# One more buffer for split weights, in place of 15 KB of descriptor scratch, in a hybrid decoder block

## The chip, the core and the metric

The kernel runs on one NeuronCore of one Trainium2 chip. The metric is the device time of one execution in microseconds. The engines are named as in the profile: PE is the matrix engine (PEld its weight loads), DVE the vector engine, ACT the scalar engine, POOL the GpSimd engine, SP the engine that issues most of the transfers. Each engine works through its own list of instructions in order, and an instruction waits until the results and the buffers that it needs are signalled ready.

## The reference, cut to what matters

The reference computes one decoder layer for 256 tokens of width 1024, in float32. A normalised input goes through one wide projection into: a gated convolution (31 taps per channel, then a layer norm, a SiLU and a projection), a sparse attention with compressed, selected and windowed branches (16 heads in 4 groups), and two gates. The gated sum is projected and added to the input. Then come a cross-attention with 4 heads into 256 memory tokens, a SwiGLU feed-forward part of inner width 2816, and a final norm.

```python
h = rms_norm(x, norm_mix_g)
x = x + hybrid_mixer(h, w_in, conv..., cmp..., w_out, rel_bias)
h = rms_norm(x, norm_x_g)
x = x + cross_attention(h, mem, xq_w, xkv_w, xo_w)
h = rms_norm(x, norm_ffn_g)
x = x + swiglu(h, ffn_in_w, ffn_out_w)
return rms_norm(x, final_norm_g)
```

Nearly all of the weights, 95 MB read from HBM in the profile, pass through the core once.

## The kernel before, in words

**The products.** A float32 matrix is split into two parts of a shorter float format (`float32r`): a high part, which is the value rounded by a copy, and a low part, which is what the copy left. A product of two matrices is then three matmuls: high by high, high by low and low by high. The activations are split once and stay. The weights are split piece by piece as they arrive.

**A piece of weight** is 128 partitions by 1024 floats, 512 KB. Three steps make it ready: SP issues its load into a buffer of the kind `w` (line 203, or 211 for the last projection), ACT copies it into a buffer of the kind `whi` (line 174, tiles named `..._0h` or `..._1h`), and DVE subtracts the copy from the loaded piece into a buffer of the kind `wlo` (line 175, tiles `..._0l`, `..._1l`). The loaded piece is free once DVE has subtracted; the two parts are free once PE has used them. Before the change there are 3 buffers of the kind `w` and 4 each of `whi` and `wlo`. A chunk such as `kw` or `f7` is two pieces, 0 and 1. Some chunks (`q0` to `q3`, `kc`) are used as loaded, in full float32 (line 269); for them PE frees the `w` buffer.

**The stages**, in the order of the program: the keys of the memory (`k0` to `k3`), the convolution's input (`u0` to `u7`), the compressed keys and values and the queries (`kc`, `vc`, `q0` to `q3`), the keys and values of the two other branches (`ks`, `kw`, `vs`, `vw`), the gates (`ga0` to `ga3`, `gc0` to `gc3`) and the memory's values (`v0` to `v3`) interleaved with the attention, the projections `pw`, `wo`, `xq`, `xo`, the feed-forward input (22 chunks `f0` to `f21`, lines 1079 and 1081) and the feed-forward output (22 pieces `fo`, line 1108).

**Convolution.** The taps of the eight channel blocks are shared out: DVE accumulates some blocks in a PSUM tile `yp` by multiply-adds (line 405), and its last one writes `part`. ACT and POOL do the others: ACT multiplies (line 419, tiles `vw_...`), POOL multiplies some (417) and adds all (421). The taps are recorded with a low priority, so that they fill time which the engines have left. The last accumulating tile `yp` and the second tile of the compressed scores (`cs_ps`, line 679) share one PSUM buffer, so PE can begin the second half of the compressed scores only after DVE's last tap.

**Order.** The order on each engine is not written out: a scheduler in the framework replays the program against its own estimate of the times and the free buffers, and fixes the order on every engine when the program is built. So a change in the number of buffers moves instructions on all engines. On PE the stages from `ks` to the end of the attention are tied down by explicit order marks (`in_line`, `last`).

## Time and profile before

| | before |
|---|---|
| median of 3 timed runs | 566.5 us (564.79 to 567.01) |
| profiled execution, first to last instruction (its span) | 563.2 us |
| PE / PEld busy | 552.7 us (98%) / 507.0 us |
| DVE / ACT / POOL busy | 426.4 / 364.0 / 136.0 us |
| granted PE clock, mean | 0.997 |
| read from HBM, mean rate | 95.39 MB, 172 GB/s with the writes |

The profile is one execution. Its span runs from the first to the last instruction on the core; the timed runs contain what lies around it too, and the profile gives no time of its own for that. The busy time of PE is modelled at the ends of the matmuls, and a matmul overlaps the next one, so the distance between two starts, not the duration, is what one costs in a row of equal ones.

### The profile page before, as it was taken

What the parts mean: (1) busy time and instruction counts of PE and PEld (TensorE: products, weight loads), DVE (VectorE), ACT (ScalarE), POOL (GpSimd) and SP (SyncE); (2) the same over time, 40 slices, a digit from 0 to 9 for tenths busy, and PEclk for the clock granted to TensorE, in tenths of its full rate; (3) what the DMA queues carried; (4) which work ended last, traced back from release to release, by engine and by line L of the source; (5) the groups of instructions that cost most, each with busy time, mean ns of one, the idle gap of its engine ahead of it and who ended that gap; (6) DMA issues with size and microseconds to landing.
All of it is one profiled execution on the core that took longest, in us unless ns stands there. A gap on an engine that the chain in (4) does not pass through costs nothing.

```text
span 563.2 us, 10246 instructions
## 1 busy us (share of the span) xinstructions
PE 552.7 (98%) x3886; PEld 507.0 (90%) x3886; DVE 426.4 (76%) x779; ACT 364.0 (65%) x686; POOL 136.0 (24%) x123
## 2 busy tenths in 40 slices
PE   8999999999999999999999999999999999999995
PEld 7999998899899998998999999988888888888884
DVE  3888999899989788886678676587787878774541
ACT  4768658878966878779556655576655666554431
POOL 0006997999982000300003100140000000000000
PEclk9999999999999999999999999999999999999998
DMA  8837924446364463432665533535565655667632
GB/s 305 355 124 263 313 55 127 133 140 216 131 208 149 154 179 104 132 105 93 251 192 179 193 120 100 181 129 186 185 200 166 218 166 166 210 190 217 190 112 74
DMA packets 29153, 97.30 MB, mean 173 GB/s; under 512 B 3120, under 2 KB 5424, under 8 KB 28848
## 3 DMA queue, kind: packets, MB, share of 16 engines
q1 hardware_dynamic: 28384, 95.34, 51.8%
q10 hardware_dynamic: 720, 1.31, 0.6%
q8 instruction: 30, 0.49, 0.3%
q14 instruction: 19, 0.16, 0.1%
HBM read 95.39 MB, written 1.25 MB: 172 GB/s over the span
## 4 chain that ended last, share of the span: by engine, by line
PE 88%; DVE 4%; ACT 3%; DMA 2%; issue 2%; ACTq 0%
PE ps_f L1079 15%; PE fo L1108 11%; PE ps_u L239 8%; PE ps_f L1081 7%; PE ps_pw L239 4%; PE ps_v L239 4%; PE ps_xq L239 4%; PE ps_wo L239 4%; PE ps_xo L239 4%; PE ps_gc L239 4%; PE ps_k L239 3%; PE ps_ga L239 3%; PE ps_q L269 3%; DVE yp L405 2%; PE s L718 2%
## 5 line engine op out<-in xcount | busy, mean ns | idle before, releaser
L421 POOL TENSOR_TENSOR yt<-yt,vw 128x512 f32<-128x512 f32 x61 | 92.3, 1514 | 54.1 <-DMA u<-in_wst_dram 46.4
L405 DVE SCALAR_TENSOR_TENSOR yp<-vt,ppt,yp 128x256 f32<-128x256 f32 x108 | 52.3, 486 | 2.9
L1079 PE MATMUL ps_f<-g,f_1h 128*128 128x512 f32 x176 | 49.0, 397 | 0.0
L419 ACT ACTIVATE vw<-vt,ppt 128x256 f32<-128x256 f32 x104 | 44.3, 497 | 5.6 <-POOL yt L421 5.5
L1079 PE MATMUL ps_f<-g,f_0h 128*128 128x512 f32 x176 | 47.7, 396 | 0.0
L1150 POOL TENSOR_SCALAR x<-x,rr 128x512 f32<-128x512 f32 x1 | 0.7, 698 | 180.9 <-DVE rr L1120 180.9
L1079 PEld LDWEIGHTS ps_f<-g,f_1h 128*128 128x128 f32 x176 | 32.6, 188 | 7.2
L175 DVE TENSOR_TENSOR f_0l<-f,f_0h 128x1024 fp32r<-128x1024 f32 x22 | 27.5, 1250 | 14.4 <-ACT f_0h L174 8.7
L1079 PEld LDWEIGHTS ps_f<-g,f_0h 128*128 128x128 f32 x176 | 30.4, 188 | 4.3
L174 ACT ACTIVATE f_1h<-f 128x1024 fp32r<-128x1024 f32 x22 | 23.2, 1055 | 14.0 <-DMA f<-in_wst_dram 14.0
L174 ACT ACTIVATE f_0h<-f 128x1024 fp32r<-128x1024 f32 x22 | 23.3, 1060 | 13.6 <-PE ps_xo L239 3.6
L175 DVE TENSOR_TENSOR f_1l<-f,f_1h 128x1024 fp32r<-128x1024 f32 x22 | 26.9, 1221 | 6.6 <-ACT f_1h L174 6.6
L1081 PEld LDWEIGHTS ps_f<-g,f_0l 128*128 128x128 f32 x176 | 27.0, 189 | 3.9
L269 PE MATMUL ps_q<-hf,q 128*128 128x256 f32 x128 | 28.5, 381 | 0.0
L1081 PE MATMUL ps_f<-g,f_0l 128*128 128x256 f32 x176 | 28.3, 282 | 0.0
L1081 PE MATMUL ps_f<-g,f_1l 128*128 128x256 f32 x176 | 28.0, 281 | 0.0
L269 PEld LDWEIGHTS ps_q<-hf,q 128*128 128x128 f32 x128 | 24.1, 190 | 3.3
L1081 PEld LDWEIGHTS ps_f<-g,f_1l 128*128 128x128 f32 x176 | 24.0, 188 | 0.0
L738 ACT ACTIVATE p<-p,mins 128x256 f32<-128x256 f32 x32 | 15.9, 498 | 9.0 <-DVE mins L723 9.0
L1082 ACT ACTIVATE ab<-ps_f 128x256 f32<-128x256 f32 x44 | 16.2, 374 | 7.2 <-PE ps_f L1081 6.9
L1083 DVE TENSOR_TENSOR ab<-ps_f,ab 128x256 f32<-128x256 f32 x44 | 17.9, 418 | 1.5 <-ACT ab L1082 1.5
L283 ACT ACTIVATE uh<-sl 128x256 fp32r<-128x256 f32 x22 | 9.1, 413 | 11.1 <-DVE sl L1087 11.1
(540 smaller groups left out, 1559.6 us busy)
## 6 DMA issues: line engine op xcount, KB each, us to landing
f<-in_wst_dram SPq DMA_DIRECT2D x44, 512.0 KB
fo<-in_wfo_dram SPq DMA_DIRECT2D x22, 512.0 KB
u<-in_wst_dram SPq DMA_DIRECT2D x14, 512.0 KB
q<-in_wst_dram SPq DMA_DIRECT2D x8, 512.0 KB
ga<-in_wst_dram SPq DMA_DIRECT2D x8, 512.0 KB
gc<-in_wst_dram SPq DMA_DIRECT2D x8, 512.0 KB
v<-in_wst_dram SPq DMA_DIRECT2D x8, 512.0 KB
pw<-in_wst_dram SPq DMA_DIRECT2D x8, 512.0 KB
```

Of the source, the lines that this page charges most:

```text
L174: copy = nc.scalar.activation(hi, w, AF.Copy)
L175: splits[name] = copy, nc.vector.tensor_tensor(out=lo, in0=w, in1=f(hi[:]), op=ALU.subtract)
L239: mm = nc.tensor.matmul(ps[:, b], lhsT=lhsT, rhs=rhs, start=row + b + kb == 0, stop=kb == NB - 1 and row == 2 and b == 1)
L269: mm = nc.tensor.matmul(ps[:, b], lhsT=w[:, k, cs], rhs=x[:, kb], start=kb + b == 0, stop=kb == NB - 1 and b == 1)
L405: nc.vector.scalar_tensor_tensor(out=out[:, i] if t == ts[-1] else acc[:, i], in0=v, scalar=w, in1=acc[:, i], op0=ALU.mult, op1=ALU.add)
L419: nc.scalar.activation(pr[:, i], v, AF.Identity, scale=w, bias=col(PP_DB, j + i) if t == 0 else 0.0)
L421: nc.gpsimd.tensor_tensor(out=y, in0=y, in1=pr, op=ALU.add)
L1079: nc.tensor.matmul(ps, lhsT=hs[kb // 4][0][:, kb % 4, cs], rhs=fg[:, :, kb], start=kb == 0, stop=False)
L1081: nc.tensor.matmul(ps[:, 1], lhsT=hs[kb // 4][1][:, kb % 4, cs], rhs=fg[:, 0, kb], start=False, stop=kb == NB - 1)
L1082: nc.scalar.activation(ab[:, b], ps[:, 0], AF.Copy)
L1083: nc.vector.tensor_tensor(out=ab[:, b], in0=ps[:, 1], in1=ab[:, b], op=ALU.add)
L1108: nc.tensor.matmul(accs[c][tb], lhsT=t, rhs=w[:, k], start=False, stop=kb == NF - 1 and t is tl)
```

## The change

The scratch that is set aside at the start of SBUF for the descriptors of dynamic transfers shrinks from 16 KB to 1 KB per partition. The 15 KB hold three more buffers of 4 KB per partition: a fourth `w`, a fifth `whi` and a fifth `wlo`. No instruction is added or removed.

```diff
     def split(w, shape, name):
-        hi = small(f"{name}h", shape, F32R, tag="whi", bufs=4)
-        lo = small(f"{name}l", shape, F32R, tag="wlo", bufs=4)
+        hi = small(f"{name}h", shape, F32R, tag="whi", bufs=5)
+        lo = small(f"{name}l", shape, F32R, tag="wlo", bufs=5)
...
-        w = small(f"{name}_{i}", [P, 4, 256], tag="w", bufs=3)
+        w = small(f"{name}_{i}", [P, 4, 256], tag="w", bufs=4)
...
     def half(src, name):
-        w = small(name, list(src.shape), tag="w", bufs=3)
+        w = small(name, list(src.shape), tag="w", bufs=4)
...
-    nc = _bacc.Bacc("TRN2", target_bir_lowering=False, num_devices=1)
+    nc = _bacc.Bacc("TRN2", target_bir_lowering=False, num_devices=1, dynamic_dma_scratch_size=1024)
```

The scheduler, given the buffers, writes another order. On PE nothing moves until the feed-forward input; on ACT and DVE the split of a piece stands about one piece earlier from the `u` chunks on.

The first place is DVE in front of the keys `kw`. `yp` is the accumulator of the taps, `ks_0l` to `kw_1l` are the low parts of the pieces, `qt` the queries from the last `q` chunk, `kcp` the compressed keys.

```order
 L284 TENSOR_TENSOR kcp<-kc_ps,kcp 128x4x16
-L405 SCALAR_TENSOR_TENSOR yp_1191<-vt_354,ppt,yp_1191 128x256 x4
-L175 TENSOR_TENSOR ks_0l<-ks_1433,ks_0h 128x1024
-L405 SCALAR_TENSOR_TENSOR yp_1191<-vt_354,ppt,yp_1191 128x256 x4
+L405 SCALAR_TENSOR_TENSOR yp_1191<-vt_354,ppt,yp_1191 128x256 x3
 L175 TENSOR_TENSOR ks_1l<-ks_1463,ks_1h 128x1024
+L405 SCALAR_TENSOR_TENSOR yp_1191<-vt_354,ppt,yp_1191 128x256
+L175 TENSOR_TENSOR kw_0l<-kw_1512,kw_0h 128x1024
+L405 SCALAR_TENSOR_TENSOR yp_1191<-vt_354,ppt,yp_1191 128x256
+L175 TENSOR_TENSOR kw_1l<-kw_1542,kw_1h 128x1024
 L405 SCALAR_TENSOR_TENSOR yp_1191<-vt_354,ppt,yp_1191 128x256
 L558 SCALAR_TENSOR_TENSOR qt<-ps_q_1381,qt 64x256
```

Both low parts of `kw` now stand ahead of the queries of the last `q` chunk; before, they stood behind them. `ks_0l` moved further up, ahead of these rows.

The second place is ACT in front of the gates. `ga_...` are the pieces of the gates (1771 and 1801 belong to `ga0`, 1836 and 1879 to `ga1`, 1964 and 2035 to `ga2`), `kdh` and `vals` hold keys and values.

```order
 L419 ACTIVATE vw_22_1507<-vt_353,ppt 128x256 x2
-L174 ACTIVATE vs_1h<-vs_1603 128x1024
-L174 ACTIVATE vw_0h<-vw_1647 128x1024
-L174 ACTIVATE vw_1h<-vw_1677 128x1024
+L174 ACTIVATE ga_0h<-ga_0_1771 128x1024
 L576 ACTIVATE kdh<-ps_kw 64x2x256 x4
+L174 ACTIVATE ga_1h<-ga_1_1801 128x1024
+L174 ACTIVATE ga_0h<-ga_0_1836 128x1024
 L592 ACTIVATE vals<-ps_vs 128x2x256
```

The first copy for the gates now stands ahead of the keys of `kw`; before, it stood behind them, behind `vals` and behind four taps more. In the same stretch, a little later, the taps end on DVE:

```order
+L405 SCALAR_TENSOR_TENSOR yp_1191<-vt_354,ppt,yp_1191 128x256 x4
+L175 TENSOR_TENSOR ga_1l<-ga_1_1879,ga_1h 128x1024
 L405 SCALAR_TENSOR_TENSOR yp_1191<-vt_354,ppt,yp_1191 128x256 x2
-L175 TENSOR_TENSOR ga_1l<-ga_1_1879,ga_1h 128x1024
-L405 SCALAR_TENSOR_TENSOR yp_1191<-vt_354,ppt,yp_1191 128x256 x3
-L405 SCALAR_TENSOR_TENSOR part_361<-vt_354,ppt,yp_1191 128x256
 L175 TENSOR_TENSOR ga_0l<-ga_0_1964,ga_0h 128x1024
-L405 SCALAR_TENSOR_TENSOR part_361<-vt_354,ppt,yp_1191 128x256
+L405 SCALAR_TENSOR_TENSOR yp_1191<-vt_354,ppt,yp_1191 128x256 x4
+L405 SCALAR_TENSOR_TENSOR part_361<-vt_354,ppt,yp_1191 128x256 x2
 L175 TENSOR_TENSOR ga_1l<-ga_1_2035,ga_1h 128x1024
```

On DVE the same instructions as before stand ahead of the last tap (`part`), in another order: `ga_0l` of `ga2` stood between its two halves and stands six multiply-adds ahead of its end now.

The third place is PE in the feed-forward input. `ps_f_0_4823` is the first half of the outputs of chunk `f4`, `ps_f_0_4766` and `ps_f_1_4785` the two halves of `f3`; the same pattern is repeated for each following pair of chunks up to `f19` and `f20`.

```order
 L1079 MATMUL ps_f_0_4823<-g_3829,f_0h 128x512 x4
+L1079 MATMUL ps_f_0_4823<-g_3829,f_1h 128x512 x4
+L1081 MATMUL ps_f_0_4823<-g_3829,f_0l 128x256 x4
 L1079 MATMUL ps_f_0_4766<-g_3829,f_0h 128x512 x4
 L1079 MATMUL ps_f_0_4766<-g_3829,f_1h 128x512 x4
 L1081 MATMUL ps_f_0_4766<-g_3829,f_0l 128x256 x4
 L1081 MATMUL ps_f_0_4766<-g_3829,f_1l 128x256 x4
+L1081 MATMUL ps_f_0_4823<-g_3829,f_1l 128x256 x4
 L1079 MATMUL ps_f_1_4785<-g_3829,f_0h 128x512 x4
 L1079 MATMUL ps_f_1_4785<-g_3829,f_1h 128x512 x4
 L1081 MATMUL ps_f_1_4785<-g_3829,f_0l 128x256 x4
 L1081 MATMUL ps_f_1_4785<-g_3829,f_1l 128x256 x4
```

Twelve of the sixteen matmuls of the later chunk's first half now stand in front of the earlier chunk; before, only four did.

## The prediction, on record before the result was known

> **What bounds the kernel now.** I read the page's busy times and its chain of waits first, then the busy time by stage, then the gaps of PE one by one, and last who ended them. From the page:

> ```profile
> span 563.2 us, 10246 instructions
> ...
> PE 552.7 (98%) x3886; PEld 507.0 (90%) x3886; DVE 426.4 (76%) x779; ACT 364.0 (65%) x686; POOL 136.0 (24%) x123
> ...
> PE 88%; DVE 4%; ACT 3%; DMA 2%; issue 2%; ACTq 0%
> ```

> The last line is the head of the chain that ended last: it runs on PE for 88%. More buffers can give back only time in which PE waits, so I look for that. The columns of the next rows (busy time in stretches of the span) are the stretch, its length, then the busy time and count of PE, PEld, DVE, ACT and POOL, the clock, the DMA share and GB/s. The last row is a stretch that I chose later: from the queries of the second `q` chunk to the end of the taps.

> ```profile
> 100.00:120.00 20.00, 20.00 (x149) 17.58 (x149) 18.18 (x43) 16.12 (x40) 18.52 (x18) 1.00 0.41 134
> 120.00:140.00 20.00, 19.11 (x146) 18.43 (x145) 19.30 (x22) 16.95 (x33) 19.27 (x15) 1.00 0.56 190
> 140.00:160.00 20.00, 18.83 (x158) 17.58 (x157) 16.92 (x21) 15.74 (x27) 19.13 (x13) 1.00 0.48 164
> 160.00:180.00 20.00, 19.33 (x162) 18.95 (x161) 18.65 (x47) 14.02 (x31) 10.09 (x6) 1.00 0.50 165
> 180.00:200.00 20.00, 20.00 (x167) 18.78 (x166) 16.97 (x59) 15.72 (x45) 0.00 (x0) 1.00 0.45 143
> ...
> 382.00:492.00 110.00, 110.00 (x629) 96.09 (x627) 85.16 (x135) 66.85 (x116) 0.00 (x0) 1.00 0.58 186
> ...
> 112.95:164.24 51.29, 48.62 (x367) 45.72 (x365) 46.73 (x63) 41.57 (x79) 47.20 (x34) 1.00 0.50 170
> ```

> PE is full at 100, from 180 on and through the feed-forward input (382 to 492). Apart from the first loads, which the change does not touch, and the end, I found gaps only from 120 to 180. There DVE (46.73 of 51.29) and POOL (47.20) are nearly full too. The gaps in PE's own timeline (start, duration, instruction, count, and in brackets the idle time before it):

> ```profile
> 129.58 1.11 PE L239 MATMUL ps_kw<-hh,kw_0h 128*128 128x256 f32 x8
> 130.53 1.11 PE L239 MATMUL ps_kw<-hl,kw_0h 128*128 128x256 f32 x8
> 132.53 1.21 PE L239 MATMUL ps_kw<-hh,kw_0l 128*128 128x256 f32 x8 [0.89 <-DVE kw_0l L175]
> ...
> 150.77 1.21 PE L239 MATMUL ps_ga<-hh,ga_0h 128*128 128x256 f32 x8 [1.02 <-ACT ga_0h L174]
> 151.82 1.10 PE L239 MATMUL ps_ga<-hl,ga_0h 128*128 128x256 f32 x8
> 153.07 1.21 PE L239 MATMUL ps_ga<-hh,ga_0l 128*128 128x256 f32 x8
> ...
> 161.04 1.19 PE L239 MATMUL ps_ga<-hh,ga_1h 128*128 128x256 f32 x8
> 162.07 0.51 PE L679 MATMUL cs_ps<-kcp,qt 128*128 128x32 f32 x4
> 162.44 1.19 PE L239 MATMUL ps_ga<-hl,ga_1h 128*128 128x256 f32 x8
> 164.29 0.62 PE L679 MATMUL cs_ps<-kcp,qt 128*128 128x32 f32 x4 [0.67 <-DVE part L405]
> ```

> Eight matmuls take 0.95 us from start to start (129.58 to 130.53). So `kw_0l` came 132.53 - 130.53 - 0.95 = 1.05 us late, `ga_0h` 1.02, and `ga_0l` 153.07 - 151.82 - 0.95 = 0.30. In front of the compressed scores the same eight took 1.85 (162.44 to 164.29) instead of 1.03 (161.04 to 162.07): 0.82. Together 3.19 us. The first three wait for split weights, the last for DVE's last tap.

> **The change, part by part.**

> *The waits for weights.* `kw_0l` is late because it stands on DVE behind the four query parts of the last `q` chunk; the new order puts it and `kw_1l` ahead of them. `ga_0h` is late because ACT makes it after eight tap multiplications; now it is made before `kdh`. Both need their loads sooner, and the fourth `w` buffer gives that:

> ```profile
> 116.51 4.45 SPq L203 DMA_DIRECT2D ks<-in_wst_dram  x2
> ...
> 124.23 1.06 ACT L174 ACTIVATE ks_1h<-ks 128x1024 fp32r<-128x1024 f32 x1 [1.63 <-DMA ks<-in_wst_dram]
> ...
> 140.72 1.06 ACT L174 ACTIVATE vw_0h<-vw 128x1024 fp32r<-128x1024 f32 x1 [2.02 <-DMA vw<-in_wst_dram]
> ...
> 146.48 3.29 ACT L419 ACTIVATE vw<-vt,ppt 128x256 f32<-128x256 f32 x8
> 149.68 1.04 ACT L174 ACTIVATE ga_0h<-ga 128x1024 fp32r<-128x1024 f32 x1
> ```

> The second load of `ks` was out by 116.51 + 4.45 = 120.96 and ACT had it at 124.23, 3.3 us later. With a buffer more every load of this stretch goes out one piece earlier. A piece keeps PE for three rows of eight, 2.85 us, so that is the lead, and ACT's waits of 1.63 and 2.02 us have cover. I expect all three waits (1.05 + 1.02 + 0.30 = 2.37 us) to go. If no load came sooner, the copies would stand where they are and the gain would be nothing; more than 2.37 there is not to have.

> *What is late next.* DVE. The second half of the compressed scores waits for `part`, the last tap, and the new order has exactly the same DVE instructions ahead of it. If PE merely arrived 2.37 us sooner it would wait that much longer there. So this part is worth what DVE's chain shortens, and DVE's timeline decides:

> ```profile
> 112.95 5.22 DVE L405 SCALAR_TENSOR_TENSOR yp<-vt,ppt,yp 128x256 f32<-128x256 f32 x10
> ...
> 130.11 2.36 DVE L175 TENSOR_TENSOR kw_0l<-kw,kw_0h 128x1024 fp32r<-128x1024 f32 x1
> ...
> 138.73 1.48 DVE L175 TENSOR_TENSOR vs_1l<-vs,vs_1h 128x1024 fp32r<-128x1024 f32 x1 [0.36 <-ACT vs_1h L174]
> 141.81 2.00 DVE L175 TENSOR_TENSOR vw_0l<-vw,vw_0h 128x1024 fp32r<-128x1024 f32 x1 [1.61 <-ACT vw_0h L174]
> ...
> 158.79 1.47 DVE L175 TENSOR_TENSOR ga_1l<-ga,ga_1h 128x1024 fp32r<-128x1024 f32 x1 [1.10 <-ACT ga_1h L174]
> ...
> 162.48 1.36 DVE L175 TENSOR_TENSOR ga_0l<-ga,ga_0h 128x1024 fp32r<-128x1024 f32 x1 [0.26 <-ACT ga_0h L174]
> 163.77 0.47 DVE L405 SCALAR_TENSOR_TENSOR part<-vt,ppt,yp 128x256 f32<-128x256 f32 x1
> ```

> The chain starts at 112.95, behind the queries of the second `q` chunk, which PE paces; a gain on DVE before that is lost in its wait for them. It ends at 163.77 + 0.47 = 164.24. DVE's waits for copies in it are 0.36 + 1.61 + 1.10 + 0.26 = 3.33 us, all behind late loads or late copies, and all have cover with the new buffers. Without them `part` ends at 160.91; PE, without its four waits, stands there at 164.29 - 3.19 = 161.10. The two chains would meet almost exactly.

> *What the splits cost there.* The price of the moved splits is the unknown. A split takes 2.36 us at 130.11 beside a busy POOL, and 1.23 in the feed-forward input, where POOL is idle. The thirteen in the chain (the row of line 175 for that stretch, whose fourteenth only begins in it), beside the two rows for comparison:

> ```profile
> 112.95:164.24 51.29, 24.00 (x14) 1.00 0.50 170
> ...
> L175 DVE TENSOR_TENSOR f_0l<-f,f_0h x22: 1215/1226/1758, 362.6 to 485.9; 128x1024 fp32r<-128x1024 f32 x22
> ...
> L421 POOL TENSOR_TENSOR yt<-yt,vw x61: 1259/1282/2615, 46.8 to 161.5; 128x512 f32<-128x512 f32 x61
> ```

> They take 24.00 / 13 = 1.85 us each. From below, all alone at 1.23, they would take 8 us less; from above, all at 2.36, 13 x 0.51 = 6.6 us more. POOL stays as full as it was, so I stay near the measured mean; but the gates' splits, of which some were short (1.47 and 1.36), move forward into POOL's busiest time. I take a tenth of the upper bound, 0.7 us, and 0.3 us for a wait that stays. Then `part` ends at 161.9, PE goes on 0.05 later as now, and the gain is 164.29 - 161.95 = 2.3 us. [...]

> *After 164.* The gain passes on if PE waits nowhere later. From 180 it has no gap now; ACT and DVE keep their order there, with one split more in hand.

> *The feed-forward input* is the one stage where PE's order changes, and PE has no wait to lose there, so it can only cost.

> ```profile
> 390.25 1.10 PE L1079 MATMUL ps_f<-g,f_1h 128*128 128x512 f32 x4
> 391.18 0.64 PE L1081 MATMUL ps_f<-g,f_0l 128*128 128x256 f32 x4
> 391.66 0.63 PE L1081 MATMUL ps_f<-g,f_1l 128*128 128x256 f32 x4
> ...
> L174 ACT ACTIVATE f_1h<-f 128x1024 fp32r<-128x1024 f32 x22 | 23.2, 1055 | 14.0 <-DMA f<-in_wst_dram 14.0
> ```

> Four matmuls take 0.93 us (390.25 to 391.18) or 0.48, so half a chunk takes 2.81 and a pair of chunks 11.25. The tightest piece is the second high part of the later chunk. Its buffer is that of `f_0h` of the pair before, free 2.81 - 0.93 = 1.88 us before that pair ends; it is now needed 0.93 us into its own pair. ACT has 2.81 us for a copy of 1.06: 1.75 us to spare. DVE has 85.16 of 110 us filled there. I cost this at nothing; what covers it is that slack, and without it each of the nine pairs waits.

> *The scratch.* I cost it at nothing. The queues and the sort of transfer:

> ```profile
> q1 hardware_dynamic: 28384, 95.34, 51.8%
> q10 hardware_dynamic: 720, 1.31, 0.6%
> ```

> Both are fed by SP and ACT; POOL issues none. [...]

> **Sum.** 563.2 - 2.3 = 560.9 for the span. The median of the runs stands 566.5 - 563.2 = 3.3 above the span, for what lies around it; with that, 564.2 us, 0.4% less than now.

> **The rivals.**

> *All four waits go.* DVE's splits cost no more than now and PE sets the pace: 3.2 us, 560.0, or 563.3 with what lies around. For it: the two chains meet within 0.2 us. Against it: every DVE wait must vanish. 22 in 100.

> *The tap chain does not shorten.* Thirteen splits that cost 0.25 us more each (of the 0.51 possible) use up the 3.33 us, and PE's earlier arrival turns into one long wait for `part`: 566.5. In the harshest form, all at 2.36, `part` ends at 160.91 + 6.6 = 167.5 and the time is 569.7. For it: DVE and POOL are both over nine tenths full there. Against it: the mean of 1.85 has that contention in it already. 19 in 100.

> *Slower: the later chunk's second copy comes late.* If ACT makes it 1 us after PE wants it in each of the nine pairs, 9 us are added: 563.2 - 2.3 + 9 + 3.3 = 573.2. It decides from a delay of 1.75 us on. For it: ACT waited 14.0 us in all for the second pieces' loads. Against it: their loads go out a piece earlier. 7 in 100.

> *The change does not do what it says*: the transfers do need the scratch and all loads slow down. For it nothing in the profile; 2 in 100.

> **How the numbers follow.** The forecast, 564.2, has the remaining 50. Its own range is 563.6 to 565.6 (a gain of 2.9 to 0.9). The range for 8 in 10 reaches to all four waits gone, less 1 us for the spread of the runs, and to no gain at all plus 1 us: 562.0 to 567.5. About 0.5% (2.8 us) is what a measurement of this kernel can tell from no change. Faster by that: the first rival and a fifth of the forecast, 0.32. Slower: the last two and the harshest form of the second, 0.1. The same: 0.58.

> **What would show it.** In the new profile PE should have no wait for `kw_0l` and `ga_0h`; the second half of the compressed scores should start at about 162 and still wait for `part`; DVE should wait less than 1 us for copies between 113 and 162; the splits there should average 1.8 to 2.0 us; and from 382 to the last matmul PE should be full. I am wrong if PE waits in the feed-forward input, or if `part` ends at 164 again.

## The result and the profile after

The changed kernel takes 560.98 us (median of 5 runs, 560.70 to 561.48). The kernel before, timed beside it, takes 566.9 us (5 runs, 564.79 to 567.84). The ratio is 0.9906, with a 95% interval of 0.9878 to 0.9934: 0.9% less. That is faster than the 564.2 us of the forecast and lies below its range, which began at 562.0.

From the page of the changed kernel, the span, the busy times and the head of the chain that ended last:

```profile
span 559.1 us, 10251 instructions
PE 552.0 (99%) x3886; PEld 507.9 (91%) x3886; DVE 426.1 (76%) x779; ACT 363.6 (65%) x686; POOL 137.5 (25%) x123
PE 99%; DVE 0%; ACT 0%; issue 0%
```

The span fell by 563.2 - 559.1 = 4.1 us while PE's busy time stayed (552.7 and 552.0). The chain was on PE for 88% and is on it for 99%; what DVE, ACT and the transfers had of it is gone. The busy time in stretches (columns as in the prediction) shows where:

```profile
120.00:140.00 20.00, 20.00 (x158) 19.57 (x157) 19.34 (x25) 18.94 (x37) 18.94 (x12) 1.00 0.66 218
140.00:160.00 20.00, 20.00 (x172) 19.05 (x171) 18.70 (x26) 17.33 (x30) 19.35 (x15) 1.00 0.60 187
160.00:180.00 20.00, 20.00 (x165) 19.66 (x164) 19.18 (x44) 12.96 (x30) 11.82 (x7) 1.00 0.45 147
...
382.00:492.00 110.00, 110.00 (x623) 95.87 (x622) 87.83 (x139) 67.44 (x119) 0.00 (x0) 1.00 0.59 191
```

PE had 19.11, 18.83 and 19.33 us in the first three and now has 20.00 in each. In the feed-forward input (the last row) it is full, as before. Its timeline at the three places of the prediction:

```profile
130.24 1.11 PE L239 MATMUL ps_kw<-hl,kw_0h 128*128 128x256 f32 x8
131.18 1.11 PE L239 MATMUL ps_kw<-hh,kw_0l 128*128 128x256 f32 x8
...
148.14 1.22 PE L239 MATMUL ps_ga<-hh,ga_0h 128*128 128x256 f32 x8
149.20 1.11 PE L239 MATMUL ps_ga<-hl,ga_0h 128*128 128x256 f32 x8
150.14 1.11 PE L239 MATMUL ps_ga<-hh,ga_0l 128*128 128x256 f32 x8
...
159.41 1.19 PE L239 MATMUL ps_ga<-hl,ga_1h 128*128 128x256 f32 x8
160.44 0.51 PE L679 MATMUL cs_ps<-kcp,qt 128*128 128x32 f32 x4
```

No PE row in this stretch has an idle time in brackets any more. The second half of the compressed scores starts at 160.44 without waiting for `part`, 1.03 us after the gate matmuls ahead of it. It stood at 164.29. DVE's side of the same meeting:

```profile
117.71 1.23 DVE L175 TENSOR_TENSOR ks_0l<-ks,ks_0h 128x1024 fp32r<-128x1024 f32 x1 [0.36 <-ACT ks_0h L174]
...
123.03 1.23 DVE L175 TENSOR_TENSOR ks_1l<-ks,ks_1h 128x1024 fp32r<-128x1024 f32 x1 [0.22 <-ACT ks_1h L174]
...
124.77 1.72 DVE L175 TENSOR_TENSOR kw_0l<-kw,kw_0h 128x1024 fp32r<-128x1024 f32 x1
...
158.30 0.87 DVE L405 SCALAR_TENSOR_TENSOR part<-vt,ppt,yp 128x256 f32<-128x256 f32 x2
```

The last tap ends at 158.30 + 0.87 = 159.17, 5.07 us sooner than before (164.24) and 1.27 us before PE asks for it. DVE waits for copies twice in this chain, 0.58 us in all, where it waited 3.33. The splits in it (their busy time in that stretch):

```profile
112.66:159.17 46.51, 22.43 (x13) 1.00 0.61 195
```

22.43 / 13 = 1.73 us each, against 1.85. The loads on SP's queue, before and then after:

```profile
124.34 0.81 SPq L203 DMA_DIRECT2D kw<-in_wst_dram  x2
```

```profile
118.97 1.72 SPq L203 DMA_DIRECT2D kw<-in_wst_dram  x2
124.28 0.80 SPq L203 DMA_DIRECT2D vs<-in_wst_dram  x2
```

`kw` goes out 5.4 us sooner, `vs` 3.7 us sooner (127.97 before). The prediction had put the lead at one piece, 2.85 us.

The median fell by 5.9 us, though, and the span of the profiled executions by 4.1. The 1.8 us between them are what the experiments had to find.

### The profile page after: what moved, and what is told of

Its sections match the earlier page's. It is cut to its first block, busy times and chain, and to the rows that moved or that the text cites. A ratio compares the mean times of both kernels' runs of the same rounds, so it can differ in the third digit from the quotient of the medians.

```text
span 559.1 us, 10251 instructions
## 1 busy us (share of the span) xinstructions
PE 552.0 (99%) x3886; PEld 507.9 (91%) x3886; DVE 426.1 (76%) x779; ACT 363.6 (65%) x686; POOL 137.5 (25%) x123
## 3 DMA queue, kind: packets, MB, share of 16 engines
q1 hardware_dynamic: 28384, 95.34, 52.8%
q10 hardware_dynamic: 720, 1.31, 0.6%
## 4 chain that ended last, share of the span: by engine, by line
PE 99%; DVE 0%; ACT 0%; issue 0%
PE ps_f L1079 15%; PE fo L1108 11%; PE ps_u L239 8%; PE ps_f L1081 7%; PE ps_q L269 5%; PE ps_ga L239 4%; PE ps_pw L239 4%; PE ps_v L239 4%; PE ps_xq L239 4%; PE ps_wo L239 4%; PE ps_xo L239 4%; PE ps_gc L239 4%; PE ps_k L239 3%; PE s L718 2%; PE ps_k L269 1%; PE pt_a L763 1%
## 5 line engine op out<-in xcount | busy, mean ns | idle before, releaser
L421 POOL TENSOR_TENSOR yt<-yt,vw 128x512 f32<-128x512 f32 x61 | 94.6, 1551 | 54.5 <-DVE yp L405 46.4
L405 DVE SCALAR_TENSOR_TENSOR yp<-vt,ppt,yp 128x256 f32<-128x256 f32 x108 | 52.2, 486 | 2.8
L419 ACT ACTIVATE vw<-vt,ppt 128x256 f32<-128x256 f32 x104 | 44.8, 498 | 10.4 <-POOL yt L421 10.1
L1079 PE MATMUL ps_f<-g,f_1h 128*128 128x512 f32 x176 | 49.0, 397 | 0.0
L1079 PE MATMUL ps_f<-g,f_0h 128*128 128x512 f32 x176 | 48.3, 396 | 0.0
L1079 PEld LDWEIGHTS ps_f<-g,f_1h 128*128 128x128 f32 x176 | 32.9, 188 | 7.5
L175 DVE TENSOR_TENSOR f_1l<-f,f_1h 128x1024 fp32r<-128x1024 f32 x22 | 27.5, 1249 | 13.4 <-ACT f_1h L174 12.4
L1079 PEld LDWEIGHTS ps_f<-g,f_0h 128*128 128x128 f32 x176 | 30.2, 188 | 4.1
L174 ACT ACTIVATE f_1h<-f 128x1024 fp32r<-128x1024 f32 x22 | 23.3, 1058 | 11.6 <-ACT ab L1082 4.4
L1081 PEld LDWEIGHTS ps_f<-g,f_0l 128*128 128x128 f32 x176 | 27.0, 189 | 3.8
L1081 PE MATMUL ps_f<-g,f_0l 128*128 128x256 f32 x176 | 28.3, 283 | 0.0
L175 DVE TENSOR_TENSOR f_0l<-f,f_0h 128x1024 fp32r<-128x1024 f32 x22 | 26.8, 1219 | 1.7 <-ACT f_0h L174 1.7
L1081 PE MATMUL ps_f<-g,f_1l 128*128 128x256 f32 x176 | 26.5, 281 | 0.0
L174 ACT ACTIVATE f_0h<-f 128x1024 fp32r<-128x1024 f32 x22 | 23.1, 1052 | 1.3 <-PE ps_xo L239 1.3
L1081 PEld LDWEIGHTS ps_f<-g,f_1l 128*128 128x128 f32 x176 | 23.3, 189 | 0.0
```

What stands on the lines that cost most here:

```text
L174: copy = nc.scalar.activation(hi, w, AF.Copy)
L175: splits[name] = copy, nc.vector.tensor_tensor(out=lo, in0=w, in1=f(hi[:]), op=ALU.subtract)
L405: nc.vector.scalar_tensor_tensor(out=out[:, i] if t == ts[-1] else acc[:, i], in0=v, scalar=w, in1=acc[:, i], op0=ALU.mult, op1=ALU.add)
L419: nc.scalar.activation(pr[:, i], v, AF.Identity, scale=w, bias=col(PP_DB, j + i) if t == 0 else 0.0)
L421: nc.gpsimd.tensor_tensor(out=y, in0=y, in1=pr, op=ALU.add)
L1079: nc.tensor.matmul(ps, lhsT=hs[kb // 4][0][:, kb % 4, cs], rhs=fg[:, :, kb], start=kb == 0, stop=False)
```

## The experiments

All are timed in five rounds beside the kernel before; its median was 566.31 us (23 runs) beside the first four, 566.23 (28 runs) beside the next four and 567.20 (11 runs) beside the last two, which ran on another chip than the other eight.

**1. The scratch alone.** The changed kernel with 3, 4 and 4 buffers again:

```diff
-        hi = small(f"{name}h", shape, F32R, tag="whi", bufs=5)
+        hi = small(f"{name}h", shape, F32R, tag="whi", bufs=4)
```

(and so for `wlo`, and 3 for `w`).

> The scratch of 1 KB alone, with the buffers of before (3, 4, 4); every engine's order of instructions is that of before. Theory (the gain comes from the buffers): as before, 566.5 to 567, within 0.3% of it, and PE waits for kw_0l, ga_0h and the last tap again, 2.5 to 4 us in all between 120 and 165. Rival (the smaller scratch itself, or where the tiles now lie in memory, does it): 561 to 562. The spans of its five runs also tell whether the wide spread of the kernel before (564.8 to 567.8) belongs to its order: if so they again spread over 2 us or more.

565.78 us, ratio 0.9998 (0.9976 to 1.0020). The scratch does nothing that 0.2% can tell. The profiled execution was one of the long ones, a span of 566.5, and it shows what the profile of before could not. PE's timeline, and then the stretches behind it (the clock is the third number from the end):

```profile
161.91 1.19 PE L239 MATMUL ps_ga<-hl,ga_1h 128*128 128x256 f32 x8
164.62 0.62 PE L679 MATMUL cs_ps<-kcp,qt 128*128 128x32 f32 x4 [1.53 <-DVE part L405]
```

```profile
164.00:166.00 2.00, 1.38 (x12) 1.38 (x13) 1.70 (x3) 0.99 (x1) 1.36 (x1) 1.00 0.37 107
166.00:168.00 2.00, 2.00 (x12) 2.00 (x11) 1.89 (x2) 0.23 (x2) 1.92 (x2) 0.56 0.86 281
168.00:170.00 2.00, 2.00 (x7) 1.61 (x7) 1.74 (x3) 1.53 (x3) 1.92 (x2) 0.50 0.77 268
170.00:172.00 2.00, 2.00 (x12) 2.00 (x11) 2.00 (x6) 0.19 (x1) 1.92 (x2) 0.50 0.67 240
172.00:174.00 2.00, 2.00 (x15) 2.00 (x15) 1.66 (x14) 2.00 (x9) 0.11 (x1) 0.73 0.53 184
174.00:176.00 2.00, 2.00 (x20) 2.00 (x19) 1.51 (x3) 2.00 (x9) 0.00 (x0) 1.00 0.27 81
```

The wait for `part` was 1.53 us here instead of 0.67, and behind it the granted clock fell to 0.50. What the clock lost is (0.44 + 0.50 + 0.50 + 0.27) x 2 = 3.4 us. "PE busy" stays at 2.00 there: a slow matmul counts as busy. Only the clock column shows it, and the time of like matmuls: eight of the scores (lines 718 and 720) take 2.71 us from 167.54 on, against 1.48 in the changed kernel.

**2. Only the fourth load buffer** (3 to 4 for `w`; `whi` and `wlo` keep 4).

> Scratch of 1 KB and only the fourth buffer for weights as loaded; high and low parts keep four. In the stretch from 112 to 165 ACT and DVE get nearly the order of the changed kernel. Theory (the earlier load is what counts): 561 to 562, with no wait of PE for kw_0l, ga_0h or the last tap; at most 1 us lost elsewhere, where the feed-forward input has another order. Rival (all three kinds are needed, a high part waits for its buffer): 564 to 567, with PE waiting for split weights.

562.33 us (562.03 to 562.85), ratio 0.9925 (0.9902 to 0.9948), a little above the 561 to 562 that I expected. Most of the gain is here, and the waits for `kw_0l` and `ga_0h` are gone. One stays; PE, and then DVE:

```profile
161.74 0.62 PE L679 MATMUL cs_ps<-kcp,qt 128*128 128x32 f32 x4 [0.62 <-DVE part L405]
```

```profile
158.60 0.48 DVE L405 SCALAR_TENSOR_TENSOR part<-vt,ppt,yp 128x256 f32<-128x256 f32 x1
159.40 1.90 DVE L175 TENSOR_TENSOR ga_0l<-ga,ga_0h 128x1024 fp32r<-128x1024 f32 x1 [0.31 <-ACT ga_0h L174]
161.22 0.47 DVE L405 SCALAR_TENSOR_TENSOR part<-vt,ppt,yp 128x256 f32<-128x256 f32 x1
```

A split stands between the two halves of the last tap, as in the kernel before. With the fifth split buffers it is done before them.

**3. Only the fifth split buffers** (`w` keeps 3).

> Scratch of 1 KB and only the fifth buffers for high and low parts; weights as loaded keep three, so the loads go out as before, and between 112 and 165 ACT and DVE keep the order of before. Theory (the earlier load counts): 565 to 567, as before, with the waits for kw_0l, ga_0h and the last tap. Rival (the split buffers were what held the copies): 561 to 563.

567.19 us, ratio 1.0006 (0.9985 to 1.0028), just above the 565 to 567 expected, with the waits for `kw_0l` (0.8), `ga_0h` (0.6) and `part` (1.34) all there, and half the clock behind the last of them. Without the earlier load the split buffers do nothing.

**4. The loads early, the splits where they stood.** The changed kernel with lines added, in the loop over the `q` chunks and behind the copy of the values:

```diff
+        if j == 3:
+            first["kw_0"] = first["kw_1"] = act, vec
...
+        if not br:
+            first["ga0_0"] = first["ga0_1"] = act,
```

> All buffers of the changed kernel, but the splits of kw are held behind the query parts of the last q chunk and those of the first gate behind the copy of the vs values, as they stood in the kernel before; the loads still go out early. If the place in the queues of ACT and DVE counts: PE waits about 1 us for kw_0l again, and 562 to 563. If the early load alone counts: no wait of PE over 0.3 us, and 561 to 561.5.

560.92 us (560.72 to 561.18), as the changed kernel. DVE has `kw_0l` behind the four query parts again, and PE does not wait:

```profile
127.95 0.43 DVE L560 SCALAR_TENSOR_TENSOR qt<-ps_q,qt 64x256 fp32r<-64x256 f32 x1
128.41 0.49 DVE L405 SCALAR_TENSOR_TENSOR yp<-vt,ppt,yp 128x256 f32<-128x256 f32 x1
128.81 1.22 DVE L175 TENSOR_TENSOR kw_0l<-kw,kw_0h 128x1024 fp32r<-128x1024 f32 x1
```

It ends at 130.03 and PE wants it at 131.18. In the kernel before the split began at 130.11 and took 2.36. So the place in the queue was not the cause: the whole queue stood later. The two prices, 1.22 and 2.36, go with what POOL did beside the split. The addition of POOL that met it, here and then in the kernel before:

```profile
128.89 2.29 POOL L421 TENSOR_TENSOR yt<-yt,vw 128x512 f32<-128x512 f32 x1
```

```profile
130.08 1.30 POOL L421 TENSOR_TENSOR yt<-yt,vw 128x512 f32<-128x512 f32 x1
```

Here the split began 0.08 us ahead of it and the addition took 2.29; before, the addition began 0.03 us ahead and the split took 2.36. Even at 2.36 the split would have ended here at 131.17, in time for PE.

**5 to 7. A wait of chosen length.** Four, six or eight idle taps (input times zero, added; the result stays the same) on DVE ahead of the last one. So that nothing else moves, the three gate splits that stand behind the last tap are held there; the third column of `eps_t` is zero. The core of the edit:

```diff
-        for t in ts:
+        for t in (*ts[:-1], *(-1,) * (2 if j == 6 else 0), ts[-1]):
...
-                v, w = vt[k][:, t:t + S], col(PP_DW + TAPS * k, t)
+                v, w = (vt[k][:, t:t + S], col(PP_DW + TAPS * k, t)) if t >= 0 else (vt[k][:, :S], eps_t[:, 2:3])
```

> The changed kernel with four idle taps (tap input times zero, added) on DVE ahead of the last tap of the chain; no other order moves there. The taps take 0.43 to 0.47 us each, the last tap ended at 159.17 and PE came at 160.44, so PE should now wait 0.5 to 0.6 us for it. Both theories: 561.4 to 561.8, and the same clock in all runs (0.997 or more), because the waits of 0.6 to 0.7 seen so far left the clock alone.

> Six idle taps: PE waits 1.3 to 1.5 us for the last tap, as long as where the clock fell in the two profiles of kernels with three load buffers. Theory (a wait of this length lets the chip halve TensorE's clock for one or two steps of some 3.4 us, and that is what spreads the kernel before): some or most runs show a clock of 0.991 to 0.995, the times spread over 2 us or more, the median is 564 to 566. Rival (a wait costs its own length and the clock's fall has another cause): 562.2 to 562.6, clock 0.997 and a spread under 1 us.

> Eight idle taps: PE waits 2.1 to 2.4 us. Theory of the clock: nearly every run falls to 0.991 to 0.994, and the time is 2.3 + 3.4 above the changed kernel, 566 to 567. Rival (length of the wait only): 563.1 to 563.5 at a clock of 0.997.

With four: 561.85 us (I expected 561.4 to 561.8), a wait of 0.30 (expected: 0.5 to 0.6), clock 0.996 to 0.999 in all 6 runs. Six: 565.76 us in the median, but in two groups: four runs of 562.42 to 562.85 at a clock of 0.997 or 0.998, and eight of 564.61 to 566.29 at 0.992 to 0.995. Eight: 566.20 us; one run of twelve, at 0.997, took 563.13, the others 564.67 to 566.69 at 0.992 to 0.996. The profiled execution with six is one of the four short runs, that with eight one of the long ones; PE's timeline and the stretches, six first:

```profile
162.18 0.62 PE L679 MATMUL cs_ps<-kcp,qt 128*128 128x32 f32 x4 [1.59 <-DVE part L405]
```

```profile
164.00:168.00 4.00, 4.00 (x32) 3.83 (x32) 4.00 (x4) 0.72 (x2) 3.92 (x3) 1.00 0.67 218
```

```profile
163.08 1.04 PE L679 MATMUL cs_ps<-kcp,qt 128*128 128x32 f32 x4 [2.12 <-DVE part L405]
```

```profile
160.00:164.00 4.00, 1.88 (x14) 1.76 (x13) 3.83 (x8) 3.23 (x5) 3.84 (x4) 0.82 0.00 1
164.00:168.00 4.00, 4.00 (x18) 3.81 (x19) 4.00 (x3) 0.60 (x1) 3.84 (x3) 0.50 0.45 141
168.00:172.00 4.00, 4.00 (x30) 3.81 (x29) 4.00 (x9) 0.01 (x1) 3.79 (x2) 0.83 0.66 216
```

The theory of the clock holds. From four idle taps to six the wait grew by 1.3 us and the median by 3.9, because eight runs of twelve paid for the clock too; in the four others the wait cost about its own length (562.42 to 562.85, against 560.98). A wait of 1.59 us does not bring the fall every time. The steps of some 3.4 us in the expectation are an estimate from the runs: against 0.998, mean clocks of 0.995 and 0.992 lose 1.7 and 3.4 of some 565 us, which at a clock of 0.50 makes a fall of 3.4 and of 6.8 us. The profiles show the long one (3.4 us lost in experiment 1); the short one is in none.

**8. The kernel before with an earlier last tap.** Three load buffers, but two taps of the last pair of blocks go from DVE to ACT and POOL:

```diff
-FIRST_G, LAST_G = 23, 10
+FIRST_G, LAST_G = 23, 12
```

> The kernel before with its three, four and four buffers and its large scratch; only two of the taps of the last pair of blocks (four of DVE's instructions, about 1.9 us) go from DVE to ACT and POOL, so that the last tap ends earlier. The weights still load late. Theory (the late last tap is what lets the clock fall): the wait for the last tap goes or stays under 0.5 us, every run has a clock of 0.997 or more, the spread shrinks to 1 us or less and the median falls to 563 to 564, 1 to 2 us still above the changed kernel for the waits for kw_0l and ga_0h. Rival (the waits for the weights do it, or something outside the kernel): the runs spread over 3 us or more as before, with clocks down to 0.992, and a median of 565.5 to 567.

564.12 us (563.12 to 565.14), ratio 0.9964 (0.9945 to 0.9983), and a clock of 0.996 to 0.999 in all twelve runs, against 0.992 in the lowest of before. PE's waits in this kernel (us in all, how many, the longest):

```profile
PE warm L337 <- DVE eps_t L157: 1.1, 1, 1.1
PE ps_kw L239 <- ACT kw_0h L174: 0.7, 1, 0.7
PE ps_vs L239 <- ACT vs_1h L174: 0.4, 1, 0.4
PE o L778 <- ACT ptt_b L766: 0.2, 1, 0.2
```

The wait for `part` is gone, and no run has a clock that low any more (one is at 0.996, where I expected 0.997 or more). Waits for weights are still there, the median is a little above the 563 to 564 that I expected, and the runs still spread over 2.0 us, twice as much as expected; what varies between them was not settled.

**9 and 10. The same two taps moved** in the kernel with only the fourth load buffer, and in the changed kernel.

> Four load buffers, four for high and low parts, small scratch (562.33 so far), and two taps of the last pair of blocks go from DVE to ACT and POOL. Theory (the fifth split buffers were worth 1.3 us only because DVE's last tap came earlier): PE no longer waits for the last tap (0.62 us before) and the time is 561.0 to 561.8, with no clock under 0.996. Rival (the fifth split buffers help at other places): 562.1 to 562.6, and PE waits elsewhere.

> The changed kernel with the same two taps moved from DVE to ACT and POOL. Theory (PE sets the pace from 20 us on, the chain of taps has 1.3 us to spare): 560.7 to 561.3, no difference. Rival (the chain of taps still costs something in some runs): 560 to 560.5. Other rival (POOL's longer chain delays the layer norm): 561.5 or more, with PE waiting for the layer norm at 200.

561.99 us (561.45 to 562.20) and 561.16 us (560.95 to 561.60). In the first PE waits for nothing but its start, as the theory said, but the median is only 0.3 below that of experiment 2 (on the other chip), where the theory had up to 1.3, and lies above the range I gave. The profiles show the wait itself gone: the second half of the compressed scores starts at 161.04, against 161.74 in experiment 2. Beside experiment 10, on the same chip, 0.8 us are left. The profiled execution is 0.6 us behind that of the changed kernel already at 30 us, and that of experiment 2 is 0.5 behind there: in both the first product (line 269, which uses no split weight) takes that much longer. Another 0.4 us is lost between 163 and 260; neither has a wait to name. So the kernel with the fifth split buffers is 1.3 us faster than the one without, of which the wait for `part` (0.62) is shown; the rest is not settled, and no profile shows that the split buffers cause it. In the second nothing is gained: the chain of taps has time to spare there. No kernel is faster than the changed one by more than the runs of one kernel differ.

## Why the prediction was wrong, point by point

*The bound and the four waits: right.* They were what there was to gain in the profiled execution. PE's place at the first gate matmuls behind the scores moved from 168.09 to 164.11, 3.98 us. By the timelines 1.06 of it is `kw_0l`, 1.09 `ga_0h`, 0.31 `ga_0l` and 0.82 the compressed scores: 3.28, against 3.19 in the prediction. Another 0.4 I had not counted: at four places, three of them behind a late operand, a group of matmuls took 0.1 us longer than its like (eight of 128x256 1.03 to 1.05 instead of 0.93 to 0.95, the four of the compressed scores 0.47 instead of 0.36). The last 0.3 us lie in the first 30 us, where PE waited 0.6 us for a first load in the profile of before; experiment 1, in the order of before, started as early as the changed kernel. They are not the change.

*"With that, 564.2 us": the step that failed.* I took 566.5 - 563.2 = 3.3 us as "what lies around" the span. It is 560.98 - 559.1 = 1.9 us after, and between 1.8 and 2.0 in each run of before and after whose span is known. The other 1.4 us were no fixed cost: the profiled execution of before was one of its short ones (563.2 + 1.9 = 565.1), and the median run had most likely lost clock. The clocks of the runs beside the prediction are not on record; the kernel before in the 28 runs beside experiments 5 to 8 had these:

| mean clock of the run | runs | time, us |
|---|---|---|
| 0.997 to 0.999 | 13 | 563.52 to 566.24 |
| 0.995 | 10 | 566.23 to 566.99 |
| 0.992 | 5 | 567.70 to 568.76 |

A loss of 0.003 of some 565 us is 1.7 us, of 0.006 is 3.4. The medians of the groups (564.6, 566.3 and 568.1) are about one and two such steps apart, and the median of all sits in the middle group. What spreads the first group over 2.7 us was not settled. So the premise that more buffers "can give back only time in which PE waits" was too narrow: they gave back clock too, which counts as busy and of which the profile of before has no loss. The hint was there: three runs of before lay 2.2 us apart, and a profile has one execution.

*"The tap chain decides": the second step that failed.* I had `part` at 161.9 and PE held by it. It came at 159.17. I had added 0.7 us to the splits and they cost 1.6 less than before (13 x 1.85 = 24.0 against 22.43); that is 2.3 of the 2.7 us. The chain began 0.3 sooner and its other instructions took 0.5 less; against that, I had left 0.3 us of waits and 0.58 stayed. Both splits of `ks` took 1.23 us, the price in the feed-forward input, where POOL is idle (0.00 of 110 us busy). Here POOL was not idle, but each split began 0.10 us ahead of an instruction of POOL. `ks_1l` began at 123.03, and the addition behind it took 2.28 us, not 1.28:

```profile
123.13 2.28 POOL L421 TENSOR_TENSOR yt<-yt,vw 128x512 f32<-128x512 f32 x1
```

The next split, `kw_0l` at 124.77, came with 0.64 us of this addition left and took 1.72, those 0.64 and 1.08 more. `kw_0l` of before came with 1.27 left, and 1.27 + 1.08 = 2.35 is its 2.36. So in these rows the price of a split follows from whether POOL's addition began before it, and how much of it is left. What makes one engine slower beside the other, no run shows. I had argued from how full POOL is and not from where each split falls. No experiment moved the splits alone, so how much of the 1.6 us the earlier loads bring and how much is luck of the new order is open. So the first rival was the true one, all four waits gone. Its span of 560.0 was 0.9 above the measured one, for the 0.4 and the 0.3 just named and 0.2 of rounding and small gains; with 1.9 us around it, it gives 561.9.

*"`kw_0l` is late because it stands behind the four query parts": wrong as a cause.* Experiment 4 has it there and PE does not wait. The late load was the cause, for the waits of the weights and for the chain of taps together; the new order followed from it. That the lead of the loads does it was right.

*The feed-forward input and the scratch: right,* at nothing. PE has 20.00 of 20 in every stretch there, and experiment 1 gives the scratch a ratio of 0.9998. What lies in the scratch, no run shows.

*The range* reached down to all four waits gone with the false 3.3 us still in it. By its own rule, 563.3 less 1, it should have begun at 562.3, not at the 562.0 that stands there. With 1.9 it would have begun at 560.9 and held the result by 0.1.

## What to carry to other kernels

Before a median and a profiled span are subtracted from one another, compare the spread of the runs with the gain that is expected: a spread of half a per cent in a kernel that PE fills is itself something to explain, and the clock of each run is the first place to look. A PE wait can have two prices, its length and what the clock does behind it (here the clock fell behind waits of 1.34, 1.53 and 2.12 us, and not behind one of 1.59 or those of up to 1.05), so a wait that hovers there is worth removing even if its own length is small. And where a chain of one engine meets PE within a few tenths, its cost has to be worked out from where each instruction falls beside those of the neighbour, not from how full that neighbour is: here a split took 1.23 us just ahead of POOL's addition and up to 2.36 just behind it.

## What the runs showed of the hardware

A split of 128x1024 on DVE took 1.22 us (experiment 4, at 128.81) or 1.23 us (the changed kernel, at 123.03) where it began 0.08 or 0.10 us ahead of an addition of POOL, which then took 2.29 or 2.28. In the kernel before, at 130.11, the addition began 0.03 us ahead; it took 1.30 and the split 2.36.
